# A mixer stage rearranged: order of the input tiles, start of the convolution chains, engine of the weight subtracts, place of the small attention steps

## The chip, the core and the metric

One core of one Trainium2 chip. The metric is device microseconds of one execution of the whole layer, taken as the median of several runs of the same program; a profile is one further execution with every instruction recorded.

## What is computed

One decoder layer on 256 tokens of width 2048, in float32: a half-step SwiGLU feed-forward block, a mixer, a second half-step SwiGLU block, each closed by a layer norm over `alpha * x + sublayer(x)`. The change lies in the mixer:

```python
u = x @ w_in + b_in                              # 2048 -> 16 q heads, 2 k, 2 v, 2 x 1024 conv
attn = softmax([q k^T / 8 (causal, window 128), sink]) v        # blocks of 128 queries
h = a * sigmoid(gate)                            # a, gate: the two conv halves of u
h = sum_k dw_w[k] * shift(h, k) + dw_b           # 31 taps, per channel, causal
conv = silu(layer_norm(h))
x = layer_norm(alpha * x + concat(attn, conv) @ w_out + b_out)
```

## The kernel before

**Matmuls in three parts.** Every float32 weight block of 128 x 1024 arrives by DMA as `raw` and is split: ScalarE casts it to `hi` (line 126), and VectorE or GpSimd subtracts `lo = raw - hi` (line 128). A product is then hi*hi + hi*lo + lo*hi. Blocks are counted by `n`; which n are subtracted on GpSimd stands in the set `pooled`, counted from the first block of the mixer (`first`). The mixer has 84 blocks: 8 of a first token group, 44 of the input projection, 16 and 16 of the two halves of the output projection. Before, GpSimd takes blocks 0, 1, 2 and 4 and four of every seven from 20 to 83.

**A planner written out by hand.** `Steps` decides, while the program is built, in what order each engine's instructions are issued; on the chip every engine then works through its own list in order. After each weight block that TensorE uses, `step()` counts one step: it runs the work that was put on `st.at(n, ...)` for that step, splits up to two blocks ahead (never more than 5 beyond those in use), and last calls `background`, which is `taps()` in the mixer. `backlog` is the planner's estimate of what VectorE still has to do: `vector(us)` adds to it, each step takes off 2.6, and `taps()` issues convolution taps while it is below `CAP` = 4.0. A tap is booked at 0.4.

**The input projection.** `ORDER` lists the tiles: a "c" is one of 8 convolution tiles (two feature blocks a and gate, 4 weight blocks, so 4 steps), a "q" one of 6 pairs of query heads (2 blocks, 2 steps); two more q pairs come with the token group. The whole takes 44 steps. In what follows c0 to c7 are the conv tiles and the "half" is the TensorE work of one weight block, 24 matmuls. At the end of a c tile `glu(i)` (line 657 on ScalarE, line 658 on VectorE) writes `hc`, which the 31 taps of that tile read. Tap 0 is on ScalarE (line 645), the other 30 are VectorE instructions (line 649); each reads `hc` from SBUF and the accumulator `conv` from PSUM and writes the accumulator back. Before, chains are begun two at a time, once two tiles are waiting, and their taps alternate; one accumulator is the single buffer of `psC`, the other one of the three buffers of `psB`, which the projections use too (tag "acc").

**Attention.** For each q pair, 2 steps after its tile, `attend(i)` writes the scores `sc` (TensorE), and puts six more pieces on later steps (`ATT`): `most` (+1; VectorE lines 687, 688, 691), `exps` (+1, ScalarE), `shares` (+2, VectorE), `divide` (+2, ScalarE), `turn` (+4, TensorE transposes into `tp`), `values` (+6), `keep` (+7; ScalarE line 736, VectorE line 737). `sc` and `tp` share the two buffers of `psA`. Before, the maxima `mx`, the negated maxima `nm` and the sink term `se` lie in SBUF.

**Around it.** `residuals` puts eight VectorE instructions (line 353) and twenty GpSimd instructions (lines 351, 357, 358) on steps 7 to 37 of the input projection. The output projection (`tokens_by`) sums over the attention rows first and over the convolution rows second; after each group of 512 columns VectorE evacuates the two sums (line 265). When no tap is left, `channel_norm` normalises the convolution (lines 778 to 801), which the second half reads.

Of the kernel before, what the change touches and what calls it, by code (L numbers as in the profile page):

```python
# [9 lines left out]
F32 = mybir.dt.float32  # L10
# [4 lines left out]
ALU = mybir.AluOpType  # L15
# [3 lines left out]
P = 128  # L19
D = 2048  # L20
S = 256
# [8 lines left out]
CK = 31  # L30
ALPHA = 2.0 ** 0.25
SCALE = 1.0 / math.sqrt(HD)
# [7 lines left out]
LEAD = 5  # L40
SKEW = 6
BC = 6
ORDER = "ccqqccqqccqqcc"
CAP = 4.0
CONV_AT = (1, 3, 1)
HB = 5
POOL_FIRST = (0, 1, 2, 4)
POOL_SPAN = (20, 84)
POOL_SHARE = (4, 7)
ZB = 5  # L50

LN_AT = ((5, 0, 0), (5, 0, 1), (6, 1, 0), (6, 2, 0), (6, 1, 1), (6, 3, 0), (6, 0, 2), (6, 2, 1), (7, 3, 1), (7, 0, 2), (7, 0, 2), (8, 0, 2))
# [128 lines left out]
def hybrid_layer(  # L181
# [3 lines left out]
    nc = tc.nc  # L185
    const = ctx.enter_context(tc.tile_pool(name="const", bufs=1))

    small = ctx.enter_context(tc.tile_pool(name="small", bufs=4))
# [3 lines left out]
    psB = ctx.enter_context(tc.tile_pool(name="psB", bufs=3, space=PSUM))  # L192
    psC = ctx.enter_context(tc.tile_pool(name="psC", bufs=1, space=PSUM))
# [14 lines left out]
    first = 2 * len(sources)  # L208
# [6 lines left out]
    items = [("w", i) for i in range(len(sources))]  # L215
    for q in range(4):
        items.insert(2 * q, ("x", q))
    pooled = {first + i for i in range(*POOL_SPAN) if i * POOL_SHARE[0] % POOL_SHARE[1] < POOL_SHARE[0]}
    for n in (first, second):
        pooled |= {n + i for i in POOL_FIRST}  # L220
    st = Steps(nc, wpool, items, sources, pooled, xT, xcat)
# [9 lines left out]
    for lo_, base, mult, step in ((0, 0, 1, -1), (P, -1, -1, 1), (2 * P, 0, 1, -1)):  # L231
        nc.gpsimd.affine_select(
            out=mask[:, lo_ : lo_ + P], in_=mask[:, lo_ : lo_ + P], compare_op=ALU.is_ge,
# [5 lines left out]
    psink = const.tile([P, NT, 2, 2], F32, name="psink")  # L239
    nsink = const.tile([P, NT, 2, 2], F32, name="nsink")  # L240
# [307 lines left out]


    x2 = mixer(tc, nc, locals())  # L550


# [17 lines left out]
def mixer(tc, nc, env):  # L570
    act, small, psA, psB, st = env["act"], env["small"], env["psA"], env["psB"], env["st"]
    xt, x1, mm3, tokens_by = env["xt"], env["x1"], env["mm3"], env["tokens_by"]
    bias, cw_sb, cp_sb, nsink, psink = (env[k] for k in ("bias", "cw_sb", "cp_sb", "nsink", "psink"))
# [3 lines left out]
    with tc.tile_pool(name="mix", bufs=1) as pool:  # L577
# [45 lines left out]
            nc.gpsimd.memset(hc[:, : CK - 1], 0.0)  # L623


        chains, todo = [], []

        def taps():
            while st.backlog < CAP:
                if not chains:  # L630
                    if len(todo) < 2:
                        return
                    for u in range(2):
                        i, hc = todo.pop(0)
                        acc = (psB.tile([P, 512], F32, tag="acc", name="conv") if u else env["psC"].tile([P, 512], F32, tag="conv", name="conv"))[:, :S]
                        chains.append([lambda k=k, i=i, hc=hc, acc=acc: tap(k, i, hc, acc) for k in range(CK)])
                for chain in chains[:]:
                    chain.pop(0)()
                    st.vector(0.4)
                    if not chain:  # L640
                        chains.remove(chain)

        def tap(k, i, hc, acc):
            if k == 0:
                nc.scalar.activation(  # L645
                    acc, hc[:, :S], AF.Identity, scale=cw_sb[:, i, 0:1], bias=cp_sb[:, 0, i : i + 1]
                )
            else:
                nc.vector.scalar_tensor_tensor(  # L649
                    out=acc if k < CK - 1 else cv[:, i], in0=hc[:, k : k + S], scalar=cw_sb[:, i, k : k + 1],  # L650
                    in1=acc, op0=ALU.mult, op1=ALU.add,
                )
# [15 lines left out]
        def attend(i):  # L668
            qT = qTs.pop(i)
            sc = psA.tile([P, 2, 512], F32, tag="gu", name="sc")  # L670
            for h in range(2):
                r = slice(h * HD, (h + 1) * HD)
                nc.tensor.matmul(sc[:, h, : 3 * P], ident_b, mask, start=True, stop=False)
                nc.tensor.matmul(sc[:, h, :P], qT[r, :P], kT[r, :P], start=False, stop=False)
                nc.tensor.matmul(sc[:, h, P : 3 * P], qT[r, P:], kT[r, :], start=False, stop=True)
            mx = small.tile([P, 2, 2], F32, tag="mx", name="mx")
            nm = small.tile([P, 2, 2], F32, tag="nm", name="nm")
            se = small.tile([P, 2, 2], F32, tag="se", name="se")
            sm = small.tile([P, 2, 2], F32, tag="sm", name="sm")
            pr = pool.tile([P, 2, 3 * P], F32, tag="pr", name="pr", bufs=2)  # L680
            pT = pool.tile([P, 2, 3 * P], F32, tag="pT", name="pT", bufs=2)
            tps = []
            st.tensor(1.6)

            def most():
                for b in range(2):
                    nc.vector.tensor_reduce(out=mx[:, b], in_=sc[:, :, spans[b]], axis=AX.X, op=ALU.max)
                nc.vector.scalar_tensor_tensor(
                    out=nm, in0=mx, scalar=-SCALE, in1=nsink[:, i], op0=ALU.mult, op1=ALU.min
                )  # L690
                nc.vector.tensor_tensor(out=se, in0=psink[:, i], in1=nm, op=ALU.add)
                st.vector(1.5)

            def exps():
                for h in range(2):
                    for b in range(2):
                        nc.scalar.activation(
                            pr[:, h, spans[b]], sc[:, h, spans[b]], AF.Exp, bias=nm[:, b, h : h + 1], scale=SCALE,
                            accum_out=sm[:, b, h : h + 1],
                        )  # L700
                nc.scalar.activation(se, se, AF.Exp)

            def shares():
                nc.vector.tensor_tensor(out=sm, in0=sm, in1=se, op=ALU.add)
                nc.vector.reciprocal(sm, sm)
                st.vector(0.3)

            def divide():
                for h in range(2):
                    for b in range(2):  # L710
                        nc.scalar.mul(pr[:, h, spans[b]], pr[:, h, spans[b]], sm[:, b, h : h + 1])

            def turn():
                tp = psA.tile([P, 2, 512], F32, tag="gu", name="tp")
                for h in range(2):
                    for n in range(3):
                        nc.tensor.transpose(
                            tp[:, h, n * P : (n + 1) * P], pr[:, h, n * P : (n + 1) * P], ident
                        )
                nc.scalar.copy(pT, tp[:, :, : 3 * P])  # L720
                st.tensor(0.7)
                tps.append(tp)

            def values():
                o = tps[0][:, :, 3 * P :]
                st.tensor(0.9)
                for h in range(2):
                    r = slice(h * HD, (h + 1) * HD)
                    nc.tensor.matmul(o[r, 0], v[0][:, r], pT[:, h, :P], start=True, stop=True)
                    nc.tensor.matmul(o[r, 1], v[0][:, r], pT[:, h, P : 2 * P], start=True, stop=False)  # L730
                    nc.tensor.matmul(o[r, 1], v[1][:, r], pT[:, h, 2 * P :], start=False, stop=True)

            def keep():
                o = tps[0][:, :, 3 * P :]
                m = [x_[:, i].rearrange("p (b n) -> p b n", b=2) for x_ in (mh, ml)]
                nc.scalar.copy(m[0], o)
                nc.vector.tensor_tensor(out=m[1], in0=o, in1=m[0].bitcast(F32), op=ALU.subtract)
                st.vector(0.35)

            for n, (work, after) in zip(  # L740
                ATT, ((most, False), (exps, True), (shares, False), (divide, True), (turn, False), (values, False), (keep, False))
            ):
                st.at(n, work, after)

        st.background = taps
        nconv, nq = 0, 2
        for kind in ORDER:
            ps = psB.tile([P, 512], F32, tag="acc", name=f"in_{kind}")
            features(ps[:, :S])
            if kind == "c":  # L750
                st.step()
                features(ps[:, S:])
                glu(nconv, ps)
                nconv += 1
                st.step()
            else:
                qTs[nq] = pool.tile([P, S], F32, tag="qT", name="qT", bufs=3)
                nc.scalar.activation(qTs[nq], ps[:, :S], AF.Identity, bias=bias[:, nq : nq + 1])
                st.at(2, lambda i=nq: attend(i))
                nq += 1  # L760
                st.step()
        while st.later and any(x_[0] - st.now < 12 for x_ in st.later):
            st.step()


        def channel_norm(b):
# [38 lines left out]


        def conv_end():
            if chains or todo:
                return taps()
            st.background = None  # L810
            channel_norm(0)
            st.at(CONV_AT[2], lambda: channel_norm(1))
# [15 lines left out]
def _layout(inputs):  # L828
# [25 lines left out]
    seq, nc_, nq = [], 0, 2  # L854
    for kind in ORDER:
        if kind == "c":
# [48 lines left out]
```

## Time and profile before

| | us |
|---|---|
| median of 3 runs | 1789.95 (1789.01 to 1790.3) |
| the profiled execution | 1786.97 |
| its span, first to last instruction | 1785.2 |
| TensorE busy in the span | 1750.2 |
| VectorE busy | 1058.7 |
| ScalarE busy | 837.8 |
| GpSimd busy | 142.2 |
| mixer, from its first matmuls to those of the next block | about 744 to 1037 |

Matmuls are pipelined, so the duration of one in the records is longer than the distance to the next. A timeline row gives the start, the time that a group of like instructions took, engine, line and operation, output and inputs, and in brackets how long the engine had been idle before and what released it.

### The profile page before, as it was taken

The page shows a single profiled execution, that of the slowest core. Times are in us where ns is not written, and L with a number is a line of the kernel's source. Part 1 is how long each engine was busy: PE and PEld are TensorE (multiplying, and loading weights), DVE is VectorE, ACT ScalarE, POOL GpSimd, SP SyncE. Part 2 cuts the span into 40 slices and gives each one's busy share as a digit, 9 for nine tenths or more (in the row PEclk, how much of TensorE's full clock was granted, in tenths as well). Part 3 has the DMA queues.
Part 4 walks back from the last instruction along what each step waited for, and adds up shares of the span by engine and source line. Part 5 has one row for each costly group of instructions (what it writes and reads, how often), then busy time and mean ns, then how long its engine had stood idle before and what let it go on. Part 6 is the DMA issues. An engine that isn't in the chain of part 4 may idle for free.

```text
span 1785.2 us, 23510 instructions
## 1 busy us (share of the span) xinstructions
PE 1750.2 (98%) x9550; PEld 1510.2 (85%) x9550; DVE 1058.7 (59%) x1386; ACT 837.8 (47%) x1145; POOL 142.2 (8%) x82
## 2 busy tenths in 40 slices
PE   8999999999999999999998999999999999999997
PEld 7888888888888888789997778888888888888885
DVE  6555555445555555658889676855544455555546
ACT  6544444334444443575653574544443334444431
POOL 0000000000000000205654420000000000000000
PEclk9999999999999999999999999999999999999999
DMA  9655555554555555445534445555555555555651
GB/s 334 236 189 189 189 189 189 193 200 175 188 189 189 189 210 190 148 163 179 179 142 165 165 165 200 215 189 189 187 201 189 193 200 189 188 188 189 223 209 48
DMA packets 52092, 336.48 MB, mean 188 GB/s; under 512 B 6288, under 2 KB 6416, under 8 KB 13072
## 3 DMA queue, kind: packets, MB, share of 16 engines
q1 hardware_dynamic: 51984, 334.98, 51.6%
q8 instruction: 75, 1.23, 0.3%
q14 instruction: 33, 0.27, 0.0%
HBM read 332.86 MB, written 2.10 MB: 188 GB/s over the span
## 4 chain that ended last, share of the span: by engine, by line
PE 95%; DVE 3%; ACT 1%; DMA 0%; issue 0%; SPq 0%; DVEq 0%
PE gu L491 35%; PE gu L497 18%; PE acc L384 10%; PE acc L386 10%; PE acc L385 10%; PE in_c L384 2%; PE in_c L385 2%; PE in_c L386 2%; PE grp L386 1%; PE grp L385 1%; PE grp L384 1%; PE in_q L384 1%; DVE z L325 1%; PE in_q L385 1%; PE in_q L386 1%; DVE conv L649 0%
## 5 line engine op out<-in xcount | busy, mean ns | idle before, releaser
L128 DVE TENSOR_TENSOR lo<-raw,hi 128x1024 fp32r<-128x1024 f32 (+1 forms) x569 | 701.9, 1240 | 234.7 <-ACT hi L126 233.6
L126 ACT CAST hi<-raw 128x1024 fp32r<-128x1024 f32 (+1 forms) x614 | 640.5, 1048 | 348.8 <-PE acc L386 319.6
L491 PE MATMUL gu<-xcat,hi 128*128 128x512 f32 x2688 | 673.1, 392 | 0.0
L491 PEld LDWEIGHTS gu<-xcat,hi 128*128 128x128 f32 x2688 | 483.7, 189 | 86.6
L497 PEld LDWEIGHTS gu<-xcat,lo 128*128 128x128 f32 x2688 | 366.7, 190 | 26.2
L497 PE MATMUL gu<-xcat,lo 128*128 128x256 f32 x2688 | 374.8, 282 | 0.0
L511 DVE TENSOR_TENSOR both<-gu,corr 128x512 f32<-128x512 f32 x84 | 58.1, 692 | 382.4 <-ACT corr L510 382.4
L384 PE MATMUL acc<-hi,hh 128*128 128x512 f32 x704 | 274.1, 389 | 0.0
L385 PE MATMUL acc<-lo,hh 128*128 128x512 f32 x704 | 273.9, 389 | 0.0
L386 PE MATMUL acc<-hi,hl 128*128 128x512 f32 x704 | 273.9, 389 | 0.0
L510 ACT COPY corr<-gu 128x512 f32<-128x512 f32 x84 | 49.2, 586 | 415.6 <-PE gu L497 415.6
L128 POOL TENSOR_TENSOR lo<-raw,hi 128x1024 fp32r<-128x1024 f32 x45 | 112.2, 2501 | 810.7 <-ACT hi L126 810.6
L386 PEld LDWEIGHTS acc<-hi,hl 128*128 128x128 f32 x704 | 132.2, 188 | 27.4
L384 PEld LDWEIGHTS acc<-hi,hh 128*128 128x128 f32 x704 | 132.2, 188 | 27.3
L385 PEld LDWEIGHTS acc<-lo,hh 128*128 128x128 f32 x704 | 132.2, 188 | 27.1
L649 DVE SCALAR_TENSOR_TENSOR conv<-hc,cw_sb,conv 128x256 f32<-128x256 f32 x232 | 93.5, 481 | 3.3 <-ACT conv L645 3.3
L384 PE MATMUL in_c<-xcat,hi 128*128 128x256 f32 x256 | 73.9, 289 | 0.0
L386 PE MATMUL in_c<-xcat,lo 128*128 128x256 f32 x256 | 72.4, 283 | 0.0
L385 PE MATMUL in_c<-xcat,hi 128*128 128x256 f32 x256 | 72.4, 283 | 0.0
L265 DVE SCALAR_TENSOR_TENSOR xt<-acc,xt 128x512 f32<-128x512 f32 x48 | 32.9, 689 | 55.9 <-PE acc L386 55.9
L384 PE MATMUL acc<-hi,mh 128*128 128x512 f32 x128 | 51.1, 399 | 7.0 <-DVE xt L265 4.6
L384 PEld LDWEIGHTS in_c<-xcat,hi 128*128 128x128 f32 x256 | 49.0, 191 | 2.4 <-issue 2.3
(125 smaller groups left out, 1121.9 us busy)
## 6 DMA issues: line engine op xcount, KB each, us to landing
raw<-in_wu SPq DMA_DIRECT2D x168, 1024.0 KB, 4.8
raw<-in_wd SPq DMA_DIRECT2D x88, 1024.0 KB, 4.7
raw<-in_win SPq DMA_DIRECT2D x26, 1024.0 KB, 4.8
raw<-in_wout SPq DMA_DIRECT2D x16, 1024.0 KB, 4.7
raw<-in_wt SPq DMA_DIRECT2D x4, 1024.0 KB, 4.7
raw<-in_wt SPq DMA_DIRECT2D x6, 512.0 KB, 6.5
xt<-in_x SPq DMA_DIRECT2D x2, 1024.0 KB, 7.7
rg<-in_rows SPq DMA_DIRECT2D x8, 256.0 KB, 5.1
```

Source lines behind the costliest of these rows:

```text
L126: nc.scalar.copy(hi, raw)
L128: eng.tensor_tensor(out=lo, in0=raw, in1=hi.bitcast(F32), op=ALU.subtract)
L265: nc.vector.scalar_tensor_tensor(out=y, in0=ps, scalar=factor, in1=y, op0=ALU.mult, op1=ALU.add)
L325: nc.vector.tensor_scalar(out=z, in0=xt[:, b, c * 512 : (c + 1) * 512], scalar1=mv[:, 0:1], scalar2=r, op0=ALU.subtract, op1=ALU.mult,)
L384: nc.tensor.matmul(ps, s_hi, m_hi, start=start, stop=False)
L385: nc.tensor.matmul(ps, s_hi, m_lo, start=False, stop=False)
L386: nc.tensor.matmul(ps, s_lo, m_hi, start=False, stop=stop)
L491: nc.tensor.matmul(gu[:, m, :], hi[:, q * P : (q + 1) * P], xc[:, k].rearrange("p a n -> p (a n)"), start=k == 0, stop=False,)
L497: nc.tensor.matmul(gu[:, m, S:], lo[:, q * P : (q + 1) * P], xc[:, k, 0, :], start=False, stop=k == KT - 1,)
L510: nc.scalar.copy(corr, gu[:, :, S:])
L511: nc.vector.tensor_tensor(out=both, in0=gu[:, :, :S], in1=corr, op=ALU.add)
L649: nc.vector.scalar_tensor_tensor(out=acc if k < CK - 1 else cv[:, i], in0=hc[:, k : k + S], scalar=cw_sb[:, i, k : k + 1], in1=acc, op0=AL ...
```

## The change

Five things. `ORDER` puts three c tiles first. Chains are kept in two lanes, each begun alone as soon as its lane is empty and a tile is waiting, lane 0 (the `psC` buffer) before lane 1 (`psB`). The GpSimd set is now blocks 8 to 51, that is the whole input projection, and of 52 to 67 those that aren't multiples of 4; 68 to 83 are all VectorE's. `mx`, `se` and a second copy `nms` of the negated maxima lie in the unused columns of the score bank in PSUM; `nm` stays in SBUF for ScalarE. And the loop that flushes later work before the output projection no longer lowers the planner's backlog.

```diff
-ORDER = "ccqqccqqccqqcc"
+ORDER = "cccqqcqqccqqcc"
-POOL_SPAN = (20, 84)
-POOL_SHARE = (4, 7)
+POOL_SPLITS = [*range(8, 52), *(i for i in range(52, 68) if i % 4)]
...
-    pooled = {first + i for i in range(*POOL_SPAN) if i * POOL_SHARE[0] % POOL_SHARE[1] < POOL_SHARE[0]}
+    pooled = {first + i for i in POOL_SPLITS}
...
-        chains, todo = [], []
+        lanes, todo = [[], []], []
+
+        def start(u):
+            i, hc = todo.pop(0)
+            ps = (
+                psB.tile([P, 512], F32, tag="acc", name="conv") if u
+                else env["psC"].tile([P, 512], F32, tag="conv", name="conv")
+            )
+            lanes[u] = [lambda k=k, acc=ps[:, :S]: tap(k, i, hc, acc) for k in range(CK)]
 
         def taps():
             while st.backlog < CAP:
-                if not chains:
-                    if len(todo) < 2:
-                        return
-                    for u in range(2):
...
-                for chain in chains[:]:
-                    chain.pop(0)()
-                    st.vector(0.4)
-                    if not chain:
-                        chains.remove(chain)
+                for u in range(2):
+                    if todo and not lanes[u]:
+                        start(u)
+                if not any(lanes):
+                    return
+                for lane in lanes:
+                    if lane:
+                        lane.pop(0)()
+                        st.vector(0.4)
...
-            mx = small.tile([P, 2, 2], F32, tag="mx", name="mx")
+            mx, nms, se = (
+                sc[:, 0, 3 * P + 4 * n : 3 * P + 4 * n + 4].rearrange("p (b h) -> p b h", b=2) for n in range(3)
+            )
             nm = small.tile([P, 2, 2], F32, tag="nm", name="nm")
-            se = small.tile([P, 2, 2], F32, tag="se", name="se")
...
-                nc.vector.scalar_tensor_tensor(
-                    out=nm, in0=mx, scalar=-SCALE, in1=nsink[:, i], op0=ALU.mult, op1=ALU.min
-                )
-                nc.vector.tensor_tensor(out=se, in0=psink[:, i], in1=nm, op=ALU.add)
-                st.vector(1.5)
+                for to in (nm, nms):
+                    nc.vector.scalar_tensor_tensor(
+                        out=to, in0=mx, scalar=-SCALE, in1=nsink[:, i], op0=ALU.mult, op1=ALU.min
+                    )
+                nc.vector.tensor_tensor(out=se, in0=psink[:, i], in1=nms, op=ALU.add)
+                st.vector(1.7)
...
         while st.later and any(x_[0] - st.now < 12 for x_ in st.later):
-            st.step()
+            st.step(0)
...
-            if chains or todo:
+            if any(lanes) or todo:
```

More of the change, by code (lines that the diff above doesn't have):

```diff
@@ L623, in mixer @@
             nc.gpsimd.memset(hc[:, : CK - 1], 0.0)
-        chains, todo = [], []
+        lanes, todo = [[], []], []
[6 more added lines that the diff above has]
+            lanes[u] = [lambda k=k, acc=ps[:, :S]: tap(k, i, hc, acc) for k in range(CK)]
         def taps():
             while st.backlog < CAP:
-                if not chains:
-                    if len(todo) < 2:
-                        return
-                    for u in range(2):
-                        i, hc = todo.pop(0)
-                        acc = (psB.tile([P, 512], F32, tag="acc", name="conv") if u else env["psC"].tile([P, 512], F32, tag="conv", name="conv"))[:, :S]
-                        chains.append([lambda k=k, i=i, hc=hc, acc=acc: tap(k, i, hc, acc) for k in range(CK)])
-                for chain in chains[:]:
-                    chain.pop(0)()
-                    st.vector(0.4)
-                    if not chain:
-                        chains.remove(chain)
+                for u in range(2):
[7 more added lines that the diff above has]
+                        st.vector(0.4)
         def tap(k, i, hc, acc):
```

## The prediction, made before the changed kernel was run

> **What bounds the kernel now.** I read the page first, then the chain of waits, then who TensorE waited for.
>
> ```profile
> PE 1750.2 (98%) x9550; PEld 1510.2 (85%) x9550; DVE 1058.7 (59%) x1386; ACT 837.8 (47%) x1145; POOL 142.2 (8%) x82
> PE 95%; DVE 3%; ACT 1%; DMA 0%; issue 0%; SPq 0%; DVEq 0%
> PE acc L384 <- DVE xt L265: 4.6, 1, 4.6
> PE acc L384 <- ACT mh L800: 2.3, 1, 2.3
> PE tp L302 <- DVE z L325: 4.7, 4, 1.9
> ```
>
> TensorE is the bound, and the change removes none of its matmuls. So the time moves only by what TensorE stands still. Two waits lie in the stage that the change touches: line 265 (it waits for a sum's buffer, behind convolution taps) and line 800 (the convolution's norm comes late). The third row lies in the layer norms, which stay. The timeline of TensorE gives the full price of the two:
>
> ```profile
> 942.51 0.39 PE L386 MATMUL acc<-hi,ml 128*128 128x512 f32 x1
> 947.53 0.47 PE L384 MATMUL acc<-hi,mh 128*128 128x512 f32 x1 [4.63 <-DVE xt L265]
> 951.17 0.47 PE L384 MATMUL acc<-hi,mh 128*128 128x512 f32 x1
> 986.58 0.39 PE L386 MATMUL acc<-hi,ml 128*128 128x512 f32 x1
> 989.30 0.50 PE L384 MATMUL acc<-hi,mh 128*128 128x512 f32 x1 [2.33 <-ACT mh L800]
> 990.30 0.50 PE L386 MATMUL acc<-hi,ml 128*128 128x512 f32 x1 [0.27 <-DVE ml L801]
> ```
>
> Undisturbed, one of these matmuls follows the other after 0.227 (48 starts from 931.83, where the projection ends, to 942.51). The first gap is 5.02, so 4.8 lost; the nine matmuls behind it take 3.64 in place of 2.04, 1.6 lost. The gap of 2.72 loses 2.5, and 0.4 more at line 801. Together **9.3 us: all that can be won.**
>
> **The change, part by part.** *Which taps alternate.* Followed through the 44 steps, the planner's counters give the order on VectorE. Before, all chains run in pairs. After, with 0.4 booked per tap, a chain is used up about when the next tile is ready: c0 starts at step 4, c1 at 8 in lane 1, and from c2 on each tile finds lane 0 empty. Only the last of c1 and first of c2 alternate, 11 taps. The other 229 taps each read what the tap directly before wrote. What does that cost?
>
> ```profile
> L649 DVE SCALAR_TENSOR_TENSOR conv<-hc,cw_sb,conv x232: 458/481/490, 804.1 to 969.1; 128x256 f32<-128x256 f32 x116
> 940.08 4.00 DVE L649 SCALAR_TENSOR_TENSOR conv<-hc,cw_sb,conv 128x256 f32<-128x256 f32 x10
> 1009.21 0.69 DVE L265 SCALAR_TENSOR_TENSOR xt<-acc,xt 128x512 f32<-128x512 f32 x1 [4.32 <-PE acc L386]
> 1009.94 0.69 DVE L268 BATCH_NORM_STATS2 stm<-xt 128x6 f32<-128x512 f32 x1
> 1010.57 0.69 DVE L265 SCALAR_TENSOR_TENSOR xt<-acc,xt 128x512 f32<-128x512 f32 x1
> ```
>
> Ten alternating taps take 4.00, so (4.00 - 0.48) / 9 = 0.391 from one to the next: each begins before the other has ended. An instruction that needs the one before it can't: line 268 reads what line 265 wrote and starts 0.04 after its end; the line 265 behind it needs nothing and starts 0.06 before. No row shows a lone chain. Its bounds are 0.391 and 0.48 + 0.04 = 0.516; I take **0.516**, since it is the dependent row's case. The Trainium skill (VectorE: DVE Perf Modes, "The DRAIN you can't avoid") says that the next VectorE instruction doesn't start until the pipe is empty, and that a semaphore costs nothing extra; by that, lone and alternating taps would cost alike (a rival below). The two line 265/268 rows don't agree.
>
> *Subtracts.* VectorE loses its splits in the projection, 27.56 us by the window below; 229 lone taps cost 229 x 0.125 = 28.6 more. The load is the same, but it sits elsewhere: VectorE starts at 787 rather than 804, and then falls behind the planner, which books 0.4 per tap.
>
> ```profile
> 785.18:931.83 146.65, 27.56 (x19) 51.25 (x21) 1.00 0.49 166
> 1028.04 6.79 DVE L325 TENSOR_SCALAR z<-xt,par 128x512 f32<-128x512 f32 x4
> 1026.66 7.43 POOL L128 TENSOR_TENSOR lo<-raw,hi 128x1024 fp32r<-128x1024 f32 x3 [7.07 <-ACT hi L126]
> 1043.78 1.92 DVE L325 TENSOR_SCALAR z<-xt,par 128x512 f32<-128x512 f32 x4
> L353 DVE TENSOR_SCALAR xt<-xt,par x16: 517/540/546, 802.5 to 1136.1; 128x512 f32<-128x512 f32 x16
> L128 POOL TENSOR_TENSOR lo<-raw,hi 128x1024 fp32r<-128x1024 f32 x45 | 112.2, 2501 | 810.7 <-ACT hi L126 810.6
> L357 POOL TENSOR_TENSOR xt<-xt,rg 128x512 f32<-128x512 f32 x8 | 10.3, 1290 | 1.0 <-DVE xt L353 1.0
> ```
>
> Four line 325 instructions take 6.79 beside GpSimd's subtracts and 1.92 without: 1.2 more each. Line 353 has that form. GpSimd will now be busy 44 x 2.5 + 20 x 1.3 = 136 of the 147 us, so each of the eight in the projection is likely to be held: between 0 (its rows) and 2.0; I take **1.0**. GpSimd itself stays in time: a block is issued four halves ahead.
>
> *Attention in PSUM.* It saves VectorE stalls beside GpSimd and adds one short instruction per pair.
>
> ```profile
> 905.52 1.25 DVE L688 SCALAR_TENSOR_TENSOR nm<-mx,nsink 128x4 f32<-128x4 f32 x1
> 913.91 0.16 DVE L688 SCALAR_TENSOR_TENSOR nm<-mx,nsink 128x4 f32<-128x4 f32 x1
> ```
>
> I count `most` at 1.5 throughout. Were it still held, it would cost at most 1.1 x 2 for each of 8 pairs, 18; the taps, one SBUF input and one from PSUM, never exceed 0.490 though GpSimd works beside them, so I take nothing.
>
> *No time:* `step(0)`, since the last `keep` falls on step 44 and nothing is left to flush. `ORDER` changes which block SP loads when, not how many, how large or at which step. VectorE's extra subtracts in the output's second half lie in its idle time ([4.32] above); without that cover they would cost some 9 x 1.14.
>
> **The sum.** TensorE's clock in the projection, by windows of its timeline (three halves; scores; transposes; values):
>
> ```profile
> 845.83:854.47 8.64, 8.64 (x74) 8.60 (x73) 7.07 (x16) 6.29 (x10) 6.60 (x4) 1.00 0.62 215
> 854.47:856.70 2.23, 2.23 (x12) 1.22 (x10) 2.23 (x7) 0.20 (x1) 2.23 (x2) 1.00 0.88 364
> 870.66:871.23 0.57, 0.57 (x9) 0.57 (x7) 0.57 (x2) 0.57 (x3) 0.00 (x0) 1.00 1.02 431
> 884.78:885.85 1.07, 1.07 (x13) 0.90 (x12) 1.07 (x3) 0.18 (x1) 1.07 (x1) 1.00 0.69 260
> ```
>
> A half is 2.88; with the joints beside attention, 40 halves, 7 scores and 8 transposes and values fill the 146.65 at 2.95, which I use. From glu to tap 1, and ScalarE's way from `exps` to the next glu:
>
> ```profile
> 785.88 0.48 DVE L658 SCALAR_TENSOR_TENSOR hc<-in_c,bias,sg 128x256 f32<-128x256 f32 x1 [2.48 <-ACT sg L657]
> 825.66 1.01 DVE L687 TENSOR_REDUCE mx<-sc 128x2 f32<-128x256 f32 x2
> 827.02 0.37 ACT L697 ACTIVATE pr<-sc,nm 128x128 f32<-128x128 f32 x1 [1.01 <-DVE nm L688]
> 830.35 1.51 ACT L711 ACTIVATE pr<-pr,sm 128x128 f32<-128x128 f32 x4
> 833.68 0.48 DVE L658 SCALAR_TENSOR_TENSOR hc<-in_c,bias,sg 128x256 f32<-128x256 f32 x1 [1.32 <-ACT sg L657]
> 932.54 0.48 DVE L658 SCALAR_TENSOR_TENSOR hc<-in_c,bias,sg 128x256 f32<-128x256 f32 x1 [1.97 <-ACT sg L657]
> 934.22 3.33 DVE L649 SCALAR_TENSOR_TENSOR conv<-hc,cw_sb,conv 128x256 f32<-128x256 f32 x8 [0.86 <-ACT conv L645]
> ```
>
> Glu's end to tap 1 is 1.2; `most` to `exps` 1.36; `exps` to glu's end 7.1, where ScalarE has the probabilities, a cast and the division in between.
>
> - c0 and c1: tap 1 at 787.6, then 54 lone taps 27.9, one `most` and `shares` 2.05, two `keep` 0.7, two line 353 at 1.46, two glu 0.9: glu2 ends at 821.9. TensorE has c2 done at 814.3 (8 halves, 1 score, 2 transposes, 2 values after 785.2). Its second q tile after that needs glu2's buffer at 820.2: **stall 1.7**.
> - Behind glu2 stand 28 taps (11 alternating, 13.1), `most`, a line 353, 3 taps, `shares`, 5 taps, `most`: `exps` of pair 3 at 843.9, pair 2's transposes **0.3** late. TensorE ends c3 at 845.0, glu3 ends at 851.0.
> - `ORDER` now has one c between two qq, so pair 4's scores need the `psA` buffer that pair 2's `keep` frees, behind 20 taps of c3: 851.0 + 1.2 + 10.3 + 0.35 = 862.9. TensorE asks for it at 856.5 (3 halves, 2 values, 1 transposes after 845.0): **stall 6.3**.
> - c4 and c5: TensorE ends c4 at 882.6, glu5 ends at 901.2; 30 taps, `keep` and two line 353 later, at 919.9, pair 6's `most`; 5.5 later, at 925.4, its probabilities. TensorE wants them at 922.2: **stall 3.2**.
> - Pair 7's `exps` then runs at 926.4, glu6 ends at 933.5 (before: 921.3). To the first evacuation: 1.2, 30 taps 15.5, `keep`, glu7, `keep` 1.2, a subtract 1.1, 22 taps 11.4, line 265 0.7: 964.6. TensorE ends c7 at 943.5, sums 512 columns in 10.9 and has half a block, 1.4, in the third `psB` buffer, free now: **stall 8.8**, and 1.6 at the slow clock.
> - The convolution ends 5 steps earlier, so the 2.9 of lines 800 and 801 go.
>
> New stalls 21.9, old 9.3: **+12.6**. Against the profiled execution's 1786.97 (span 1785.2 and 1.8 around it) that is 1799.6; the runs' median lies 3.0 higher, so 1802.6. With line 353 held by nothing the sum is +8, with 2.0 each +18. The Trainium skill (TensorE: Matmul & The Clock Gate, "Part 1: The HAM clock gate") halves the clock after about 3.4 us of idling; the gaps of 5.02 and 2.72 agree. By it the 6.3 stall too would cost some 1.6 more, +14.2.
>
> **The rivals.** *Faster: the lone chain costs no more than a pair.* Then glu2 isn't late: the 54 taps may take up to 0.393 each before it is. Only some 1.8 of the evacuation's stall stays; -7.5, 1782.5. For it: VectorE is free 17 us sooner. Against it: the dependent rows. *No change: the stalls in the projection are absorbed*, say because VectorE makes up its lag before pair 4. Then glu6 ends at 921.3, the evacuation at 952.4 against 944.1: 8.3 + 1.6 - 9.3 = +0.6, 1790.5. *GpSimd becomes the bound*: its multiplies wait for line 353 in VectorE's late list; eight times 3 makes 160 us against 147 + 11.5 of stalls, and if the lead is used up TensorE waits 2 to 6 more: 1806. *The change doesn't free VectorE*: that is the forecast's own case, by the load above.
>
> **How the numbers follow.** Forecast 0.63, faster 0.15, no change 0.16, GpSimd 0.06. A difference of 0.2%, 3.6 us, is about what a measurement of this kernel can tell from none. Faster than that: 0.17; within: 0.14; slower: 0.69. The range, 1785 to 1809, leaves out most of the faster rival and the far end of the held line 353; the forecast's own is 1796 to 1809.
>
> **What would show it.** Lone taps 0.51 apart; line 353 above 0.54; TensorE waiting at line 673 for line 737, at line 717 for line 711, and still at line 384 for line 265, with no wait for line 800. It is wrong if lone taps step at 0.39, or if the lag at glu2 is under 1 us.

## The result, and the profile after

| | before | after |
|---|---|---|
| median, us (range) | 1789.48 (1787.54 to 1790.3) | 1810.74 (1809.43 to 1811.61) |
| the profiled execution, us | 1786.97 | 1811.61 |
| its span, us | 1785.2 | 1809.8 |

The changed kernel takes 1.0119 times as long (95% interval 1.0107 to 1.0132), 21.3 us more; four runs of each were made. The forecast was +12.6, and its range ended at 1809. The sign and the place were right, the size was not. The profiled execution of the kernel before lies 2.5 under its median and that of the changed kernel 0.9 above, so the two profiles differ by 24.6.

First the same lines of the page as before: busy time by engine, the chain of work that ended last, and the groups of splits and taps (count | busy us, mean ns | idle before).

```profile
PE 1761.2 (97%) x9550; PEld 1518.4 (84%) x9550; DVE 1054.3 (58%) x1375; ACT 838.4 (46%) x1145; POOL 181.0 (10%) x101
PE 89%; DVE 6%; ACT 1%; issue 1%; POOL 1%; DMA 0%; SPq 0%; DVEq 0%; POOLq 0%
L128 POOL TENSOR_TENSOR lo<-raw,hi 128x1024 fp32r<-128x1024 f32 x64 | 153.3, 2409 | 845.1 <-ACT hi L126 839.1
L654 DVE SCALAR_TENSOR_TENSOR conv<-hc,cw_sb,conv 128x256 f32<-128x256 f32 x232 | 112.7, 489 | 10.3 <-ACT conv L650 3.2
```

TensorE runs the same 9550 matmuls and is busy 11 us longer: some of them ran slower. VectorE's share of the chain has doubled, from 3% to 6%. Its own busy time hardly moved, as forecast. So its totals tell nothing; the order of its list does. Next, who TensorE waited for between 800 and 1010 us (total, times, longest):

```profile
PE acc L384 <- DVE xt L265: 7.2, 1, 7.2
PE sc L678 <- DVE ml L745: 6.1, 1, 6.1
PE tp L725 <- ACT pr L719: 3.7, 1, 3.7
PE zt L798 <- DVE cv L790: 2.3, 1, 2.3
PE in_q L384 <- DVE hc L663: 1.4, 1, 1.4
```

The old waits of 4.6 and 2.3 have become five. (Line numbers are each kernel's own: line 654 is the old 649, 663 the old 658, 678 the old 673, 719 the old 711, 745 the old 737.) VectorE's timeline shows where it is late, start and duration first:

```profile
822.38 0.48 DVE L663 SCALAR_TENSOR_TENSOR hc<-in_c,bias,sg 128x256 f32<-128x256 f32 x1
851.15 0.48 DVE L663 SCALAR_TENSOR_TENSOR hc<-in_c,bias,sg 128x256 f32<-128x256 f32 x1 [3.97 <-ACT sg L662]
852.63 10.46 DVE L654 SCALAR_TENSOR_TENSOR conv<-hc,cw_sb,conv 128x256 f32<-128x256 f32 x20 [1.00 <-ACT conv L650]
863.00 0.42 DVE L745 TENSOR_TENSOR ml<-tp,mh 128x256 fp32r<-128x256 f32 x1
938.10 0.49 DVE L663 SCALAR_TENSOR_TENSOR hc<-in_c,bias,sg 128x256 f32<-128x256 f32 x1 [4.46 <-ACT sg L662]
957.84 11.51 DVE L654 SCALAR_TENSOR_TENSOR conv<-hc,cw_sb,conv 128x256 f32<-128x256 f32 x22
969.25 1.28 DVE L265 SCALAR_TENSOR_TENSOR xt<-acc,xt 128x512 f32<-128x512 f32 x2
```

Twenty taps in 10.46 us are (10.46 - 0.49) / 19 = 0.525 from start to start, against 0.391 when two chains alternate. The `keep` of line 745 stands behind these twenty in the list, and TensorE's scores for pair 4 wait for it. The first evacuation, line 265, stands behind another 22.

The waits are only part of it. TensorE's timeline around three of them, and the windows behind them (start:end, length, then busy time of PE, PEld, DVE, ACT and POOL, TensorE's granted clock, DMA share, GB/s):

```profile
863.47 0.48 PE L678 MATMUL sc<-mask,ident_b 128*128 128x384 bf16 x1 [6.13 <-DVE ml L745]
867.47 0.58 PE L384 MATMUL in_q<-xcat,hi 128*128 128x256 f32 x1
871.68 0.28 PE L384 MATMUL in_c<-xcat,hi 128*128 128x256 f32 x1
929.47 1.78 PE L725 MATMUL tp<-ident,pr 128*128 128x128 f32 x6 [3.66 <-ACT pr L719]
962.39 0.39 PE L386 MATMUL acc<-hi,ml 128*128 128x512 f32 x1
969.99 0.79 PE L384 MATMUL acc<-hi,mh 128*128 128x512 f32 x1 [7.21 <-DVE xt L265]
975.70 0.57 PE L385 MATMUL acc<-lo,mh 128*128 128x512 f32 x1
```

```profile
863.47:867.47 4.00, 4.00 (x10) 1.96 (x10) 3.75 (x8) 0.00 (x0) 1.70 (x2) 0.50 0.60 193
929.47:938.66 9.19, 9.19 (x54) 8.65 (x54) 1.38 (x7) 9.13 (x22) 8.02 (x4) 0.69 0.35 121
969.99:975.70 5.71, 5.71 (x13) 4.46 (x14) 5.46 (x10) 1.04 (x1) 1.62 (x1) 0.50 0.53 174
996.73:999.44 2.71, 2.71 (x9) 2.12 (x8) 2.45 (x2) 2.29 (x6) 1.76 (x1) 0.50 0.03 6
```

After each of the four waits the granted clock is 0.50 for some microseconds. The scores block of 2.23 takes 4.00 and the half behind it 4.21 (867.47 to 871.68) in place of 2.95: 3.0 lost. The transposes and two halves take 9.19; at 0.57 and two halves of 2.96 they are 6.5: 2.7 lost. Thirteen matmuls take 5.71 where 13 x 0.227 is 2.95: 2.8 lost. Behind the fourth wait, the one of 2.3 at the transposes of the convolution's norm, the same stretch begins; counted over the gaps there that are too long, from the transposes to 1000.15, it costs 1.7.

So the books of the profiled executions, each wait as the lengthening of a gap between two starts of TensorE (as the prediction took them; the evacuation's is 969.99 - 962.39 - 0.227 = 7.4), each slow stretch as the lengthening of the gaps behind it:

| | predicted | measured |
|---|---|---|
| wait for glu2 (line 663) | 1.7 | 1.6 |
| pair 2's transposes | 0.3 | 0 |
| scores of pair 4 behind `keep` | 6.3 | 6.2 |
| pair 6's probabilities | 3.2 | 3.8 |
| first evacuation (line 265) | 8.8 | 7.4 |
| transposes of the convolution's norm | none | 2.4 |
| slow clock behind four of these | 1.6 | 3.0 + 2.7 + 2.9 + 1.7 = 10.3 |
| old waits and slow clock, gone | -9.3 | -9.3 |
| sum | +12.6 | +22.4 |

The third slow stretch is the 2.8 above and one more slow gap. The wait of 2.4 is the idle time of 2.3 of the wait row and the little by which the gap around it is longer. The two profiled executions differ by 24.6, 2.2 more than the table. Ahead of the mixer, in code that the change doesn't touch, the same transposes already start 1.3 later, before (first) and after:

```profile
736.53 0.63 PE L302 MATMUL tp<-ident,z 128*128 128x128 f32 x4
```

```profile
737.80 0.63 PE L302 MATMUL tp<-ident,z 128*128 128x128 f32 x4
```

The rest, 0.9, lies behind the mixer; the layer norm there has a slow stretch too (a mean clock of 0.93, where the same norm before had 1.00):

```profile
1053.00:1078.00 25.00, 21.38 (x100) 16.71 (x99) 20.16 (x31) 19.24 (x44) 7.29 (x3) 0.93 0.38 126
```

### The profile page after: what moved, and what is told of

Same layout as the page of the kernel before. It is cut to its first block, busy times and chain, and to the rows that moved or that the text cites. A ratio compares the mean times of both kernels' runs of the same rounds, so it can differ in the third digit from the quotient of the medians.

```text
span 1809.8 us, 23513 instructions
## 1 busy us (share of the span) xinstructions
PE 1761.2 (97%) x9550; PEld 1518.4 (84%) x9550; DVE 1054.3 (58%) x1375; ACT 838.4 (46%) x1145; POOL 181.0 (10%) x101
## 4 chain that ended last, share of the span: by engine, by line
PE 89%; DVE 6%; ACT 1%; issue 1%; POOL 1%; DMA 0%; SPq 0%; DVEq 0%; POOLq 0%
PE gu L491 34%; PE gu L497 18%; PE acc L384 10%; PE acc L385 10%; PE acc L386 10%; DVE conv L654 3%; PE in_c L384 1%; PE in_c L385 1%; PE in_c L386 1%; PE grp L386 1%; PE grp L385 1%; PE grp L384 1%; POOL lo L128 1%; DVE z L325 1%; DMA raw<-in_wt 0%
## 5 line engine op out<-in xcount | busy, mean ns | idle before, releaser
L128 DVE TENSOR_TENSOR lo<-raw,hi 128x1024 fp32r<-128x1024 f32 (+1 forms) x550 | 668.2, 1221 | 226.3 <-ACT hi L126 224.6
L128 POOL TENSOR_TENSOR lo<-raw,hi 128x1024 fp32r<-128x1024 f32 x64 | 153.3, 2409 | 845.1 <-ACT hi L126 839.1
L654 DVE SCALAR_TENSOR_TENSOR conv<-hc,cw_sb,conv 128x256 f32<-128x256 f32 x232 | 112.7, 489 | 10.3 <-ACT conv L650 3.2
```

The costliest lines, as they stand in the source:

```text
L128: eng.tensor_tensor(out=lo, in0=raw, in1=hi.bitcast(F32), op=ALU.subtract)
L654: nc.vector.scalar_tensor_tensor(out=acc if k < CK - 1 else cv[:, i], in0=hc[:, k : k + S], scalar=cw_sb[:, i, k : k + 1], in1=acc, op0=AL ...
```

## The experiments

Two theories were set against each other. By the first (L in the expectations), chains begun singly make each tap wait for the one before it; VectorE's list then runs late at the points where TensorE needs it, and TensorE's clock falls behind each stall. By the second the order of the tiles (O), the GpSimd set (G) or the steps in PSUM cost the time. The kernel before, measured beside these runs, had medians of 1789.4 to 1790.2; each ratio is to it.

### The changed kernel with the old pairs of chains

```diff
-        lanes, todo = [[], []], []
...
+        chains, todo = [], []
...
+                    if len(todo) < 2:
+                        return
+                    for u in range(2):
```

> The changed kernel with the chains begun in pairs again, all else as changed. Theory L (a lone chain steps at 0.52 us per tap where a pair steps at 0.39; VectorE falls behind, TensorE stalls and its clock drops): VectorE has 28 us less to do than before the change, so no lag; the waits for line 265 and for the keep step shrink below 2 us each and the time is 1780 to 1790. Theory O (the new tile order alone causes it, by the score buffer and the bunched attention): the wait of the scores for the keep step stays near 6 us and the time is 1800 or more. Theory G (GpSimd's subtracts hold VectorE or come late): 1800 or more.

Measured: 1786.19, ratio 0.9982 (0.9973 to 0.9991). All taps alternate again. TensorE's waits in the stage:

```profile
PE acc L384 <- DVE xt L265: 2.2, 1, 2.2
PE acc L384 <- ACT mh L803: 1.9, 1, 1.9
PE sc L673 <- DVE ml L740: 0.4, 1, 0.4
```

One part undone takes away the whole loss and 3 us more. The other four parts together are a small gain.

### Only the single chains, in the kernel before

```diff
-        chains, todo = [], []
+        lanes, todo = [[], []], []
+
+        def start(u):
...
```

> The kernel before with nothing changed but that chains are begun singly. Theory L: VectorE keeps its 27.6 us of subtracts and gets some 28 us of slower taps on top, so it is later than in the changed kernel: 1805 to 1830. Theories O and G: within 3 us of before, or faster, as the convolution starts 15 us earlier.

Measured: 1804.01, ratio 1.0082 (1.0065 to 1.0099).

```profile
PE in_q L384 <- DVE hc L663: 8.0, 2, 4.6
PE acc L384 <- DVE hc L663: 7.8, 1, 7.8
```

The single chains cost some 14.6 us alone, and 24.6 where the other parts are present (1810.74 against 1786.19). Here other instructions of VectorE's list are the late ones: three times a glu that stands behind taps. Which wait it becomes depends on what is queued there; that it becomes one doesn't. The time lies just under the range expected.

### Is it the dependence? Two sums for each tile

Even and odd taps go into two accumulators, so that neighbours don't depend on each other although one chain runs alone. Tap 1 moves to ScalarE, and one addition joins the sums. First both sums lie in the two halves of one PSUM buffer:

```diff
+            accs = (ps[:, :S], ps[:, S:])
+            lanes[u] = [lambda k=k: tap(k, i, hc, accs[k % 2], accs[1]) for k in range(CK)]
...
+            elif k == 1:
+                nc.scalar.activation(acc, hc[:, 1 : 1 + S], AF.Identity, scale=cw_sb[:, i, 1:2])
...
+                if k == CK - 1:
+                    nc.vector.tensor_tensor(out=cv[:, i], in0=cv[:, i], in1=other, op=ALU.add)
```

> The changed kernel, but each chain adds its even and its odd taps into two sums (the two halves of its PSUM bank), joined at the end by one more add; tap 1 goes to ScalarE. No tap needs the one right before it. Theory L: taps step at 0.39 again, the lag at the third conv tile is under 2 us, the time is 1779 to 1789. Theories O and G: 1805 or more, as nothing that they name is changed. If the two halves of one bank count as dependent, the taps still step at 0.52 and it tells nothing.

Measured: 1810.57, ratio 1.012 (1.0105 to 1.0135). Its taps lie as far apart as in the changed kernel, by VectorE's timeline:

```profile
788.29 4.69 DVE L657 SCALAR_TENSOR_TENSOR conv<-hc,cw_sb,conv 128x256 f32<-128x256 f32 x9 [1.50 <-ACT conv L655]
```

That is (4.69 - 0.49) / 8 = 0.525. This run neither supports nor refutes the theory, since the pace that it was to change did not change. So the sums were put into two buffers, the even taps in `psC`'s and the odd ones in one of `psB`'s, and one tile at a time is worked on:

```diff
+            accs = (
+                env["psC"].tile([P, 512], F32, tag="conv", name="conv")[:, :S],
+                psB.tile([P, 512], F32, tag="acc", name="conv")[:, :S],
             )
...
-                for u in range(2):
-                    if todo and not lanes[u]:
-                        start(u)
+                if todo and not lanes[0]:
+                    start(0)
```

> The changed kernel with one chain at a time, begun singly, whose even taps add into the buffer of psC and whose odd taps add into one of psB, joined by one more add; tap 1 goes to ScalarE. Unlike the two halves of one bank, two banks count as independent. Theory L (dependent taps): taps step at 0.39, no wait of the scores for the keep step above 2 us, 1779 to 1788. If it isn't the dependence but the early single start, or that one lane alone works: 1800 or more.

Measured: 1788.56, ratio 0.9992 (0.9983 to 1.0002), a hair above the time expected. A row of VectorE's timeline:

```profile
789.56 3.63 DVE L655 SCALAR_TENSOR_TENSOR conv<-hc,cw_sb,conv 128x256 f32<-128x256 f32 x9 [0.92 <-ACT conv L649]
```

The waits of TensorE in the same kernel:

```profile
PE zt L801 <- DVE cv L793: 2.3, 1, 2.3
PE acc L384 <- DVE cv L660: 1.8, 1, 1.8
```

Now (3.63 - 0.49) / 8 = 0.392, and no wait is longer than 2.3. The chains are still begun singly, as in the changed kernel, and 22 us are gone. So it is not the single start that costs the time but neighbouring taps on one PSUM buffer. With both sums in one buffer no tap needs the result of the one before it, and they lie 0.525 apart all the same: sharing the buffer is enough. Whether needing the result would be enough by itself was not tried.

### Is it the pace, or a plan that doesn't know it?

```diff
-                        st.vector(0.4)
+                        st.vector(0.4 if all(lanes) else 0.52)
```

> The changed kernel, but the planner books 0.52 for a tap when one lane alone is at work (0.4 as before when both are). Theory L with the planner's part in it: fewer taps are issued ahead of the attention's steps, tiles pile up, both lanes work more often; the wait of the scores for the keep step falls below 4 us; 1786 to 1800. If only the pace of the taps matters and not what is issued ahead of what: within 4 us of the changed kernel.

Measured: 1789.77, ratio 0.9997 (0.9987 to 1.0006), as fast as before. TensorE's waits, and the row of `keep` in VectorE's timeline:

```profile
PE acc L384 <- DVE hc L663: 3.3, 1, 3.3
PE acc L384 <- DVE xt L265: 3.0, 1, 3.0
```

```profile
855.03 0.42 DVE L745 TENSOR_TENSOR ml<-tp,mh 128x256 fp32r<-128x256 f32 x1
```

Most taps are still alone here (156 lone, 56 alternating, counted in the trace; 210 and 11 in the changed kernel). But the planner, told what a lone tap takes, puts fewer of them ahead of each attention step: the `keep` that TensorE waited for at 863.00 runs at 855.03. Against the version with pairs (1786.19), in which the other four parts are the same, it is 3.6 slower, and the two intervals just overlap. So of the 24.6 that the single chains cost there, the booking gives back 21.0. Part of this is pace, since 54 fewer taps are alone; how much was not separated. The loss needs both, taps of 0.525 and a plan that books them at 0.4: with either one put right, nearly all of it is gone.

### The clock behind the stalls

Here the changed kernel gets extra matmuls, whose results nobody reads, ahead of three of its stalls: 24 before pair 4's scores, 13 before pair 6's transposes, 28 before the wait for the first evacuation. The stalls stay; TensorE is not idle in them.

```diff
+        def warm(n, of, tag):
+            t = of.tile([P, 2 if of is psA else 1, 512], F32, tag=tag, name="warm")
+            for _ in range(n):
+                nc.tensor.matmul(t[:, 0], x1[:, 0, 0, :P], x1[:, 0].rearrange("p a n -> p (a n)"), start=True, stop=True)
...
+            if i == 4:
+                warm(24, psB, "acc")
...
+                if i == 6:
+                    warm(13, psB, "acc")
...
+                if warm is not None and (c, t) == (1, 0):
+                    warm(28, psA, "gu")
```

> The changed kernel with matmuls put into three of TensorE's stalls whose results nobody reads: 24 of 512 columns (5.4 us) ahead of pair 4's scores, 13 (2.9) ahead of pair 6's transposes, 28 (6.4) ahead of the first half block that waits for line 265. They fit into the waits, so by themselves they cost nothing. Theory C (what the stalls cost beyond their length is the clock, which drops because TensorE idled): the slow stretches of 3.1, 2.7 and 2.9 us behind the three go, and the time falls by 6 to 9 us, to 1802 to 1805. If the clock drops for another reason: 1809 to 1813.

Measured: 1806.23, ratio 1.009 (1.0075 to 1.0105), 4.5 us under the changed kernel, less than the 6 to 9 expected. TensorE's timeline, windows and waits:

```profile
857.85 5.74 PE L678 MATMUL warm<-xcat 128*128 128x512 f32 x24
864.05 0.32 PE L689 MATMUL sc<-mask,ident_b 128*128 128x384 bf16 x1 [0.46 <-DVE ml L758]
```

```profile
863.00:868.00 5.00, 4.54 (x27) 3.12 (x26) 4.72 (x11) 0.00 (x0) 2.88 (x2) 1.00 0.45 152
929.00:939.00 10.00, 10.00 (x88) 9.70 (x87) 3.15 (x7) 9.94 (x23) 6.30 (x5) 1.00 0.57 203
969.00:976.00 7.00, 7.00 (x28) 5.64 (x27) 4.07 (x9) 2.10 (x2) 3.71 (x2) 0.87 0.42 150
```

```profile
PE acc L384 <- DVE xt L265: 4.4, 2, 2.9
```

The scores start at the same point as without the fill (864.05 against 863.47), but at full clock, and so do the transposes. Ahead of the evacuation the fill was too short: 2.9 idle remained, and some of the slow stretch with it. The last row also holds a second, new wait for line 265 of 4.4 - 2.9 = 1.5, which took part of the gain back. That the slow stretches come from the idling, and are paid on top of the wait, is shown by the first two windows.

### The other parts, one at a time

The changed kernel with the old order of tiles:

```diff
-ORDER = "cccqqcqqccqqcc"
+ORDER = "ccqqccqqccqqcc"
```

> The changed kernel with the old tile order. Theory O: the 6 us wait of the scores for the keep step and what follows go, 1792 or less. Theory L: chains are still lone, VectorE still late; stalls elsewhere, 1796 to 1812. Theory G: as the changed kernel, near 1810.

Measured: 1807.51, ratio 1.0102 (1.0087 to 1.0117). The wait of pair 4's scores for `keep` is gone, as the prediction's argument from the order says. Others took its place, by the waits:

```profile
PE acc L384 <- DVE xt L265: 9.8, 2, 8.3
PE tp L725 <- ACT pr L719: 7.4, 2, 4.3
```

The new order alone, in the kernel before:

```diff
-ORDER = "ccqqccqqccqqcc"
+ORDER = "cccqqcqqccqqcc"
```

> The kernel before with the new tile order alone, chains in pairs. Theory L: pairs keep VectorE on time, so at most a wait of 2 us of the scores for the keep step: 1787 to 1793. Theory O (the order itself): 1795 or more.

Measured: 1794.63, ratio 1.0033 (1.002 to 1.0046): 4.4 us, more than the 1787 to 1793 expected. Among TensorE's waits the old two are as they were, and one is added:

```profile
PE sc L673 <- DVE ml L737: 2.0, 1, 2.0
```

These 2.0 explain less than half of it. The rest goes with the clock: the mean granted clock of its five executions is 0.992 to 0.994, that of the twenty of the kernel before 0.994 to 0.997. The kernel with the PSUM steps alone (below) has the clock at 0.50 in the same three places and for as long (3.4, 6.8 and 3.4 us). Its profiled execution took 1790.82 against 1793.39 here, so at like clock 2.6 remain, near the wait. With pairs, the new GpSimd set and the PSUM steps beside it (the first experiment) this wait shrinks to 0.4, so the order costs little there.

The new GpSimd set alone, in the kernel before:

```diff
-POOL_SPAN = (20, 84)
-POOL_SHARE = (4, 7)
+POOL_SPLITS = [*range(8, 52), *(i for i in range(52, 68) if i % 4)]
```

> The kernel before with the new set of GpSimd subtracts alone. Theory L: VectorE has less to do and chains still run in pairs, 1783 to 1790. Theory G (GpSimd's subtracts hold VectorE at lines 353, 688, 691 or come late): 1793 or more.

Measured: 1787.07, ratio 0.9987 (0.9978 to 0.9997). Among TensorE's waits the one for line 265 falls from 4.6 to 2.2, with fewer splits left to VectorE, and GpSimd does not become the bound:

```profile
PE acc L384 <- DVE xt L265: 2.2, 1, 2.2
```

The small attention steps in PSUM alone, in the kernel before:

```diff
-            mx = small.tile([P, 2, 2], F32, tag="mx", name="mx")
+            mx, nms, se = (
+                sc[:, 0, 3 * P + 4 * n : 3 * P + 4 * n + 4].rearrange("p (b h) -> p b h", b=2) for n in range(3)
+            )
...
+                for to in (nm, nms):
```

> The kernel before with the small attention steps in PSUM alone. Theory L: it removes stalls of 2 to 3 us of VectorE in all, off TensorE's path: 1786 to 1791. Were the PSUM accesses themselves the cause (maxima written beside the scores): 1795 or more.

Measured: 1789.64, ratio 1.0 (0.999 to 1.0009). No difference, as expected.

### The norm of the convolution later, and the fastest version

`CONV_AT` sets at which steps of the output projection the planner puts the three parts of the convolution's norm. In the changed kernel, with the second two steps later:

```diff
-CONV_AT = (1, 3, 1)
+CONV_AT = (1, 5, 1)
```

> The changed kernel with the convolution's swish put two steps later (CONV_AT's middle number 5 for 3); the norm now ends five steps before it is needed. If the wait of 2.3 us at the second zt transposes comes from the norm's second half standing one step too close ahead of them on VectorE, it goes, and with it the slow stretch of 2 us behind it: 1805 to 1808. If VectorE is late there for the taps' sake, the wait stays or moves to the second half's first matmul: 1809 to 1812.

Measured: 1807.59, ratio 1.0101 (1.0086 to 1.0116), 3.2 under the changed kernel. The wait at the norm's transposes is gone, and there is no slow stretch around it, by the window there (a second wait for line 265, of 1.1, is new):

```profile
982.00:998.00 16.00, 15.99 (x79) 13.11 (x78) 14.52 (x33) 6.31 (x9) 7.75 (x3) 1.00 0.47 181
```

So removing the fourth stall and the slow stretch behind it gained about 3, the new wait included. The same edit on the version with two sums in two buffers:

> One chain at a time with its taps in two banks, and the swish two steps later. By the same reasoning 4 us under the kernel with two banks alone, so 1782 to 1787, which would be below before. If the norm isn't the cause of that wait: 1787 to 1790.

Measured: 1786.68, ratio 0.998 (0.997 to 0.9989). It is 1.9 under the same version without the edit, less than the 4 hoped for; the wait at the transposes is gone here too, and one of 1.1 for line 265 is new. This version, the first experiment and the new GpSimd set alone lie 0.1 to 0.2% under the kernel before, with intervals that leave out 1 and overlap one another.

## Why the prediction was wrong in size

**What bounds, and where.** Right. 22.5 of the 24.6 between the profiles arise in the mixer, from TensorE's standing still and from what follows it, in the projection and in the output projection behind it. The three waits that the prediction named are there, and the one for line 800 is not.

**Which taps are alone, and their price.** Right. 229 lone taps were forecast, 210 are lone and 11 alternate in the trace (the others begin a run behind another instruction). They lie 0.525 apart; 0.516 was taken, from the dependent pair of lines 265 and 268. The Trainium skill (VectorE: DVE Perf Modes, "The DRAIN you can't avoid") says that the next VectorE instruction does not start before the pipe has emptied; it adds, which the prediction left out, that one that is not held starts earlier. Read whole, it does not make the two cases alike, and the runs don't either: 0.392 with two sums in two buffers, 0.525 with one. The rival that rested on equal prices falls with that.

**The subtracts.** Right: VectorE's load stayed (1058.7 to 1054.3), and GpSimd did not become the bound. Line 353 was held by 0.8 on average, against the 1.0 taken; the group of its rows (min/median/max in ns):

```profile
L353 DVE TENSOR_SCALAR xt<-xt,par x16: 539/541/2248, 805.7 to 1161.4; 128x512 f32<-128x512 f32 x16
```

The longest of the sixteen took 2.248, 0.54 is its undisturbed length, and the eight in the projection average 1.36 in the trace.

**Attention in PSUM, `step(0)`, the later subtracts, the loads.** Costed at nothing. For the PSUM steps that is shown (a ratio of 1.0 alone); `step(0)` was not tried alone, and the later subtracts only within the whole GpSimd set. The order of the tiles was costed as loads at nothing and as the wait of pair 4 within the walk; alone, it cost 4.4, of which the wait made 2.0.

**The walk along VectorE's list.** Right to a microsecond in the first half, some 5 us too early in the second; 1.3 of each difference is the later start ahead of the mixer. Glu2 was to end at 821.9 and ended at 822.9, glu3 at 851.0 and 851.6, `keep` of pair 2 at 862.9 and 863.4. Glu6 was to end at 933.5 and ended at 938.6, the first evacuation at 964.6 and 969.9, by the start of the matmul that waited for it. The five stalls that were forecast sum to nearly the same, 19.0 against 20.3, since TensorE had fallen back as well; with both sides late, that agreement is in part luck. The glu rows of 851.15 and 938.10 show VectorE idle for 4 us ahead, waiting for ScalarE: so there it was not its own list that was late, but what it was given; that this was TensorE's delay handed on, slow stretches included, is a reading of these rows and was not tested.

**The failed step: the slow clock, counted once and at 1.6.** The sum had 1.6 of it, behind the evacuation, from the old stall of 5.0. It comes behind every stall of 3.7 and more, and costs more each time: 3.0, 2.7, 2.9 and, behind the unforeseen 2.4, another 1.7. That is 8.7 more than the sum had; the table's sums differ by 9.8, with 2.4 for the unforeseen wait and 1.3 less for the others. The size was wrong beside the count. Behind the old stall the clock stayed at 0.50 for 3.4 us, by the window of the kernel before:

```profile
947.91:951.32 3.41, 3.41 (x10) 2.64 (x9) 3.41 (x8) 0.00 (x0) 0.00 (x0) 0.50 0.40 163
```

Behind the three long stalls of the changed kernel it stayed there for 6.8, 5.7 and 6.1 us after TensorE had started again, and half of each is about what was lost.

The Trainium skill (TensorE: Matmul & The Clock Gate, "Part 1: The HAM clock gate") was cited for the stall of 6.3 alone, at 1.6; the trace agrees with it that an idle stretch longer than 3.4 us halves the clock, three times over. The stall forecast at 3.2 turned out at 3.8 and was followed by it as well. With 1.6 behind each of the three the sum would have been +15.8, still short. The sentence early in the working that the time moves only by what TensorE stands still was where it went wrong: it also moves by how slowly TensorE starts again.

**The smaller miss: the norm's 2.9.** Lines 800 and 801 were to have their cover because the convolution ends five steps earlier. It did not end earlier, since VectorE was late. The last tap of each tile writes `cv`; the group of these in the line view, before and after:

```profile
L649 DVE SCALAR_TENSOR_TENSOR cv<-hc,cw_sb,conv x8: 468/471/474, 840.9 to 969.9; 128x256 f32<-128x256 f32 x8
```

```profile
L654 DVE SCALAR_TENSOR_TENSOR cv<-hc,cw_sb,conv x8: 476/481/482, 808.2 to 975.2; 128x256 f32<-128x256 f32 x8
```

The last one starts at 975.2, against 969.9. Line 800's wait did go, but the transposes of the norm got one of 2.3 in its place. The experiment with the norm two steps later gains 3.2 by removing this wait and the slow stretch behind it.

**The other cases.** No change was given 0.16 on the ground that VectorE might make up its lag; it did not, but under a plan that books 0.52 the loss does go. Faster and the GpSimd bound are refuted by the pace and by the waits.

## What to carry over

Before single chains replace alternating ones, find the distance of two dependent instructions in the trace (a row that reads what the row before it wrote), and change the planner's booked price with it: here the right price alone gave back 21 of the 24.6 us that single chains cost. Where a change puts TensorE to wait, count the wait and the slow matmuls behind it, once for each wait of several microseconds; here that was about half as much again as the waits themselves. A wait of about 2 us may bring them or not, as the last section shows. And if chains must run alone, give each two sums in separate buffers.

## What was unexpected of the hardware

Two accumulators in one PSUM buffer, 256 columns each, are as slow as one (0.525); in two buffers the taps lie 0.392 apart. What makes the halves of a buffer depend on each other, the chip or the waits put into the program, was not separated.

The length of a gap does not decide alone whether the clock falls. The gap of 2.3 at the norm's transposes was followed by a slow stretch in the changed kernel; the changed kernel with the old order had the same wait of 2.3, at the same line, and none. The clock records show what differs. In each of the fourteen profiles the granted clock falls only at instants that lie whole multiples of 3.41 us apart, and apart from the one at the program's end every slow stretch lasts one, two or three such steps. In the changed kernel the gap, 993.54 to 995.82, lies within one step, and the clock is at 0.50 for the next (the window of 996.73 above). The step with the gap:

```profile
993.14:996.55 3.41, 1.13 (x9) 0.76 (x8) 3.27 (x8) 2.79 (x6) 0.51 (x1) 1.00 0.45 190
```

With the old order the gap, 990.41 to 992.71, is cut in two by the end of a step, and the clock stays at 1.00:

```profile
988.72:992.13 3.41, 1.69 (x8) 1.06 (x6) 3.09 (x12) 3.35 (x9) 0.00 (x0) 1.00 0.76 298
992.13:995.55 3.42, 2.84 (x17) 2.53 (x18) 3.42 (x3) 2.43 (x6) 2.48 (x1) 1.00 0.03 7
```

Over the fourteen profiles, up to the program's end, the clock fell 40 times. No step at full clock in which TensorE was idle for less than 1.78 us was followed by a fall, and every one with more than 1.93 was. So a gap of 2 us costs nothing or up to 1.7, half a step, by where the steps happen to lie, and they lie elsewhere in each execution. Of twenty executions of the kernel before, the six with a mean granted clock of 0.997 took 1787.2 to 1788.4 us, the fourteen with 0.994 or 0.995 took 1789.4 to 1791.3. A forecast of a wait of about 2 us is uncertain by as much again.
